# Attention values with both parts of V in one stationary operand, and the post-norm weights loaded when the norm chain begins

## The chip, the cores and the metric

The kernel runs on one core of a Trainium2 chip. The metric is the device time of one execution in microseconds (us), the median over several runs. The engines are TensorE (PE, with its weight loads listed apart as PEld), VectorE (DVE), ScalarE (ACT), GpSimd (POOL) and SyncE (SP), which issues most DMAs.

## What is computed

The reference is a trunk of two layers on 512 tokens of width 1024. Layer 0 has a pooling and state-space mixer, layer 1 has neighbourhood attention on a grid of 8 rows by 64 columns, and each layer has a feed-forward block ahead of the mixer or attention and one behind it. So there are six blocks in a row: ffn0, mixer, ffn1, ffn2, attention, ffn3. Every block is wrapped in two root-mean-square norms, and the second (the post-norm, with weights `norm_g[layer, k]`) is applied to the block's output before it is added to the residual stream:

```python
def rms_norm(x, g):
    y = xf * lax.rsqrt(jnp.mean(xf * xf, axis=-1, keepdims=True) + RMS_EPS)
    return (y * g.astype(F32)).astype(x.dtype)
...
        s = jnp.einsum('bqhd,biqjhd->bhqij', q_r, k_nb).astype(F32) + bias[None]
        p = jax.nn.softmax(s.reshape(bsz, N_HEADS, GRID_W, kh * KW), axis=-1)
...
        return jnp.einsum('bhqij,biqjhd->bqhd', p, v_nb)
```

There are 16 heads of 64 dimensions.

## The kernel before

**Products in parts.** Every fp32 matrix is split into a rounded part `hi` and a rest `lo`. A product is made of three products of parts, all summed in one PSUM bank: hi·hi, hi·lo and lo·hi (`mm3`, whose three lines are L170, L171 and L172). The split is made by `split_evac`: ACT copies PSUM into `hi` (L385), and DVE subtracts that from PSUM into `lo` (L386). With `later` the DVE half is put on a list and emitted afterwards. Weights come by DMA into `w_raw` (L74), ACT casts them to `w_hi` (L113), and DVE (or POOL) makes `w_lo` (L124).

**Attention.** Tokens stand in four query tiles of 128 for each head, so there are 64 units (head, tile `t`). A query tile sees a set of 192 or 256 keys, and its 128-key pieces are the two `CHUNKS` of the tile. One loop of 69 slots runs over the units as a pipeline. Slot by slot it emits, in this order: what `later` holds, `normalize` of the unit before, `values` of the unit five back, `transpose` of the unit three back, `scores` of this unit, one step of `spread` (evacuation of q and k), and then on average 1.35 filler steps on PE (`FILL_RATE`; projections of v, q and k for later heads, and products of the output projection, in banks `ps_f`). `scores` makes the logits in `ps_qk` (L883, L884), adds the bias, and takes the exponential; `transpose` turns the probabilities through PE (L907, bank `ps_pt`) and splits them into `pt_hi` and `pt_lo`; `values` multiplies them with `v_hi` and `v_lo` into `ps_o`. For each unit that is two chunks of three products with a 64-column stationary piece of V (one head) and 128 moving query columns. Some chunks have 64 keys, so that their products use 64 rows of the array. At `t == 3` the head's `ps_o` is split into `oT_hi` and `oT_lo`, the input of the output projection.

**The end of a block.** The output projection of a block is made in two halves of 512 columns: `ps_A` and then `ps_B` (in attention the first half stands in `ps_f` and `ps_o`). When the first half is done, a pool `chain` is allocated where the block's working tiles stood, and `chain_begin` takes the tile `fg` from it. `post_pair` sums the squares of each tile of 128 tokens on ACT (the tile `junk`) and multiplies it by `gpost` on DVE (`fg`, L242). Four more weight tiles (the tail) are split then, for the products of the second half, whose `fg` follow. Then come the residual, the norm of the next block, and its transposed input `xT_hi`, `xT_lo` (L319), on which the next block's products wait.

**The post-norm weights.** `load_gpost` broadcasts one row of 1024 weights to 128 partitions (512 KB in SBUF) by a DMA on SP's queue. It is called at the start of each block, and `gpost` stands in the pool `base`, which lives through the whole kernel.

Of the kernel before, what the change touches and what calls it, by code (L numbers as in the profile page):

```python
# [7 lines left out]
F32 = mybir.dt.float32  # L8
F32R = mybir.dt.float32r
# [6 lines left out]
P = 128  # L16
D = 1024
# [145 lines left out]
class Builder:  # L163
# [55 lines left out]

    def load_gpost(self, layer, k):  # L220
        self.gpost = self.base.tile([P, D], F32, tag="gpost", bufs=1, name="gpost")
        self.nc.sync.dma_start(self.gpost, self.ins["norm_g"][layer, k].partition_broadcast(P))
# [4 lines left out]

    def chain_begin(self, pool, scale):

        self.c_pool, self.c_scale = pool, 1.0 / (32.0 * scale)  # L230
        self.c_eps = EPS / (scale * scale)
        self.fg = pool.tile([P, TT, D], F32, name="fg")
        self.c_ss = {}
# [314 lines left out]
    def ffn(self, layer, which, gain, nxt, before, ssm=None):  # L548
# [5 lines left out]
        tc, nc, V = self.tc, self.nc, self.nc.vector  # L554
        self.load_gpost(layer, 1 if which == 0 else 5)
        n_plain = N_PLAIN[0 if ssm else 1]
# [188 lines left out]
    KEY0 = (0, 64, 192, 320)  # L745
    NKEY = (192, 256, 256, 192)

    CHUNKS = (((0, 64, 0, 64), (64, 128, 1, 0)), ((0, 128, 1, 0), (128, 128, 2, 0)),
              ((0, 128, 2, 0), (128, 128, 3, 0)), ((0, 128, 3, 0), (128, 64, 0, 0)))

    def attention(self, nxt, before):
        tc, nc, V = self.tc, self.nc, self.nc.vector
        ins = self.ins
        self.load_gpost(1, 3)
# [10 lines left out]
        def load_bias(head):  # L765
            bias[head] = z["ap"].tile([P, 4, 256], F32, tag="bias", bufs=2, name="bias")
            nc.sync.dma_start(bias[head], ins["att_bias"][head])
# [48 lines left out]
        def v_steps(c):  # L816

            pv = [self.bank("ps_f") for _ in range(2)]
            for i in range(2):
                w = self.W.take()  # L820
                for j in range(4):
                    kt = 4 * i + j
                    for s in range(4):
                        o = s % 2 * 256
                        self.mm3(pv[s // 2][:, o:o + 256], [keys(x[:, kt, :], s) for x in self.xT_all],
                                 [x[:, j * 256:(j + 1) * 256] for x in w], kt == 0 and s % 2 == 0,
                                 kt == KT - 1 and s % 2 == 1)
                    if kt < KT - 1:
                        yield
                if i == 0:  # L830
                    self.W.done()
            for b, ps in enumerate(pv):
                hi, lo = (x[:, 2 * b:2 * b + 2, c * 256:(c + 1) * 256] for x in vt)
                self.split_evac(hi, lo, ps.rearrange("p (s n) -> p s n", s=2), None, later)
            self.W.done()
            yield
# [38 lines left out]
        def scores(u):  # L875
            hp, a, t = u // 8, u // 4 % 2, u % 4
            rows, n = slice(64 * a, 64 * a + 64), self.NKEY[t]
            ps = self.bank("ps_qk")
            while u % 8 == 0 and spread:
                run_spread()  # L880
            tq = q[hp][a][:, t * P:(t + 1) * P]
            hi, lo = (x[:, self.KEY0[t]:self.KEY0[t] + n] for x in (k[hp][a], k[hp][2]))
            nc.tensor.matmul(ps[:, :n], tq, hi, start=True, stop=False)  # L883
            nc.tensor.matmul(ps[:, :n], tq[rows], lo[rows], start=False, stop=True)  # L884
            p = ap.tile([P, 256], F32, tag="p", bufs=5, name="p")
            m, s = self.small("att_m", 1), self.small("att_s", 1)
            V.tensor_tensor_reduce(out=p[:, :n], in0=ps[:, :n], in1=bias[2 * hp + a][:, t, :n], scale=-1.0,
                                   scalar=3e38, op0=ALU.add, op1=ALU.min, accum_out=m)
# [12 lines left out]
        def transpose(u):  # L901
            p, _ = st[u]
            ps = self.bank("ps_pt")
            pt = [ap.tile([P, 2, P], F32R, tag="pt" + n, bufs=2, name="pt" + n) for n in ("_hi", "_lo")]
            ch = self.CHUNKS[u % 4]
            for c, (o, n, _, _) in enumerate(ch):
                nc.tensor.transpose(ps[:n, c * P:(c + 1) * P], p[:, o:o + n], self.ident)  # L907
            if ch[0][1] == ch[1][1]:
                self.split_evac(pt[0], pt[1], ps[:, :256].rearrange("p (c n) -> p c n", c=2), None, later)
            else:  # L910
                for c, (_, n, _, r) in enumerate(ch):
                    self.split_evac(pt[0][r:r + n, c], pt[1][r:r + n, c], ps[:n, c * P:(c + 1) * P],
                                    None, later)
            st[u] = pt
# [404 lines left out]
    def mixer(self, nxt, before):  # L1319
        tc, nc, V, G = self.tc, self.nc, self.nc.vector, self.nc.gpsimd  # L1320
        ins = self.ins
        self.load_gpost(0, 3)
        xh, xl = self.xT
# [274 lines left out]
        cp = tc.alloc_tile_pool(name="chain", bufs=1)  # L1598
        self.chain_begin(cp, 1.0)
        out_a(range(TT), (4, 5))  # L1600
# [135 lines left out]
def lay_out(inputs):  # L1736
# [16 lines left out]
    for t in range(4):  # L1753
# [7 lines left out]
    bias = bias.reshape(16, 4, P, 256).transpose(0, 2, 1, 3)  # L1761

# [53 lines left out]
```

## Time and profile before

| what | value |
|---|---|
| median of three runs | 1896.97 us (1895.35 to 1897.27) |
| the profiled execution's own time | 1898.08 us |
| its span in the profile | 1896.3 us |
| granted TensorE clock, mean | 0.994 |
| PE busy | 1834.5 us, 97% |
| PEld busy | 1642.3 us, 87% |
| DVE busy | 1471.5 us, 78% |
| ACT busy | 925.5 us, 49% |
| POOL busy | 350.2 us, 18% |

Busy times are sums over the whole span. What an engine costs at one place has to be read from that place: an instruction's row has its start, its length, and in brackets the idle time of its engine before it and what ended that.

### The profile page before, as it was taken

To read this page: it belongs to the slowest core of one execution; us is meant where nothing else is said; L and a number is where in the kernel's file an instruction comes from. 1 tells how busy PE (TensorE), PEld (TensorE's weight loads), DVE (VectorE), ACT (ScalarE), POOL (GpSimd) and SP (SyncE) were. 2 spreads that over 40 slices of the span, in tenths; PEclk is the share of its full clock that TensorE was granted. 3 is DMA by queue.
4 is the path that set the end of the run, shared out by engine and by line. 5 is a ranking of instruction groups with operands and counts; after the bars stand their busy time and mean duration, and the time that the engine had idled before them with its cause. 6 is when DMAs were issued, how large, how long until landed. Compare 5 with 4: busy or idle time off the path is not lost.

```text
span 1896.3 us, 31539 instructions
## 1 busy us (share of the span) xinstructions
PE 1834.5 (97%) x12368; PEld 1642.3 (87%) x12368; DVE 1471.5 (78%) x2380; ACT 925.5 (49%) x1749; POOL 350.2 (18%) x238
## 2 busy tenths in 40 slices
PE   7999998998899999999999999999999999999998
PEld 7877996887679999988899998889878789999886
DVE  5788989968769999854899996465565579999744
ACT  5344446365455454543644445355555565444532
POOL 2021231014011223200132330002222012322100
PEclk9999999999999999999999999999999999999999
DMA  5365336637532333332233323223222132333321
GB/s 195 127 198 188 101 123 199 206 120 253 172 123 79 101 112 101 106 115 80 79 111 104 108 90 133 90 78 129 85 99 100 57 111 90 101 112 101 122 93 64
DMA packets 82021, 225.48 MB, mean 119 GB/s; under 512 B 15792, under 2 KB 20048, under 8 KB 80848
## 3 DMA queue, kind: packets, MB, share of 16 engines
q1 hardware_dynamic: 70176, 197.80, 31.0%
q0 software_dynamic: 6960, 23.57, 4.1%
q10 hardware_dynamic: 4736, 2.10, 0.4%
q8 instruction: 97, 1.59, 0.3%
q14 instruction: 52, 0.43, 0.1%
HBM read 206.69 MB, written 18.84 MB: 119 GB/s over the span
## 4 chain that ended last, share of the span: by engine, by line
PE 65%; DVE 5%; ACT 3%; issue 1%; DMA 1%; DVEq 0%; ACTq 0%
PE ps_gu L172 10%; PE ps_gu L171 10%; PE ps_gu L170 10%; PE ps_A L170 3%; PE ps_A L172 3%; PE ps_A L171 3%; PE ps_B L172 3%; PE ps_B L171 3%; PE ps_B L170 3%; PE ps_f L170 3%; PE ps_f L171 2%; PE ps_f L172 2%; PE ps_qk L884 1%; ACT junk L226 1%; DVE w_lo L124 1%
## 5 line engine op out<-in xcount | busy, mean ns | idle before, releaser
L124 DVE TENSOR_TENSOR w_lo<-w_raw,w_hi 128x1024 fp32r<-128x1024 f32 x214 | 283.4, 1330 | 210.7 <-ACT w_hi L113 210.6
L113 ACT CAST w_hi<-w_raw 128x1024 fp32r<-128x1024 f32 (+1 forms) x313 | 262.8, 864 | 264.5 <-PE ps_A L172 73.7
L172 PE MATMUL ps_gu<-xsum,w_lo 128*128 128x256 f32 x1088 | 308.1, 283 | 0.8 <-DVE w_lo L124 0.8
L171 PE MATMUL ps_gu<-xsum,w_hi 128*128 128x256 f32 x1088 | 308.2, 283 | 0.3 <-DVE xsum L505 0.3
L172 PE MATMUL ps_gu<-xT_hi,w_lo 128*128 128x256 f32 (+1 forms) x1008 | 307.1, 305 | 1.4 <-DVE w_lo L124 1.4
L170 PE MATMUL ps_gu<-xsum,w_hi 128*128 128x256 f32 x1088 | 307.8, 283 | 0.0
L170 PE MATMUL ps_gu<-xT_hi,w_hi 128*128 128x256 f32 (+1 forms) x1008 | 304.9, 303 | 0.0
L171 PE MATMUL ps_gu<-xT_lo,w_hi 128*128 128x256 f32 (+1 forms) x1008 | 304.6, 302 | 0.0
L172 PEld LDWEIGHTS ps_gu<-xsum,w_lo 128*128 128x128 f32 x1088 | 208.8, 192 | 0.9 <-DVE w_lo L124 0.9
L171 PEld LDWEIGHTS ps_gu<-xsum,w_hi 128*128 128x128 f32 x1088 | 208.6, 192 | 0.7 <-DVE xsum L505 0.7
L170 PEld LDWEIGHTS ps_gu<-xsum,w_hi 128*128 128x128 f32 x1088 | 208.6, 192 | 0.0
L172 PEld LDWEIGHTS ps_gu<-xT_hi,w_lo 128*128 128x128 f32 x1008 | 190.5, 189 | 12.7 <-DVE w_lo L124 2.2
L170 PEld LDWEIGHTS ps_gu<-xT_hi,w_hi 128*128 128x128 f32 x1008 | 190.4, 189 | 8.5 <-issue 0.9
L171 PEld LDWEIGHTS ps_gu<-xT_lo,w_hi 128*128 128x128 f32 x1008 | 190.3, 189 | 7.3
L98 POOL TENSOR_TENSOR w_u<-w_raw,w_s 128x512 f32<-128x512 f32 x64 | 112.2, 1753 | 360.9 <-ACT w_hi L113 196.3
L124 POOL TENSOR_TENSOR w_lo<-w_raw,w_hi 128x1024 fp32r<-128x1024 f32 x31 | 74.0, 2389 | 564.0 <-ACT w_hi L113 533.9
L113 ACT CAST w_hi<-w_s 128x512 fp32r<-128x512 f32 x136 | 77.8, 623 | 197.8 <-DVE w_s L96 192.8
L96 DVE TENSOR_TENSOR w_s<-w_raw,w_u 128x1024 f32<-128x1024 f32 x68 | 145.8, 2144 | 2.4
L172 PE MATMUL ps_A<-w_hi,gT 128*128 128x512 f32 x352 | 138.3, 393 | 5.7 <-DVE gT L678 5.7
L625 POOL TENSOR_TENSOR g<-g,m 128x1024 f32<-128x1024 f32 x34 | 94.6, 2781 | 245.0 <-DVE m L623 245.0
L170 PE MATMUL ps_A<-w_hi,gT 128*128 128x512 f32 x352 | 138.0, 392 | 1.1 <-DVE m L620 1.1
L171 PE MATMUL ps_A<-w_lo,gT 128*128 128x512 f32 x352 | 137.8, 392 | 0.0
(376 smaller groups left out, 4259.0 us busy)
## 6 DMA issues: line engine op xcount, KB each, us to landing
w_raw<-in_w_gu_dram SPq DMA_DIRECT2D x106, 512.0 KB, 3.3
w_raw<-in_w_dn_dram SPq DMA_DIRECT2D x88, 512.0 KB, 3.2
w_u<-in_w_gu_dram SPq DMA_DIRECT2D x70, 512.0 KB, 3.7
w_raw<-in_w_qk_dram SPq DMA_DIRECT2D x16, 512.0 KB, 3.2
bias<-in_att_bias_dram SPq DMA_DIRECT2D x16, 512.0 KB, 4.1
w_raw<-in_w_in_dram SPq DMA_DIRECT2D x8, 512.0 KB, 3.2
cm<-m_dram SPq DMA_DIRECT2D x4, 1024.0 KB, 8.0
w_raw<-in_w_ao_dram SPq DMA_DIRECT2D x8, 512.0 KB, 3.8
```

Of the source, the lines that this page charges most:

```text
L96: tt(out=blocks(s), in0=g[:, :HALF].unsqueeze(1).broadcast_to([P, 2, HALF]), in1=blocks(u)[:, :2], op=ALU.subtract)
L98: (h_engine or self.nc.gpsimd).tensor_tensor(out=u[:, :HALF], in0=g[:, HALF:], in1=s[:, HALF:], op=ALU.add)
L113: self.nc.scalar.copy(hi[:, k:k + step], src[:, k:k + step])
L124: (engine or self.lo_engine).tensor_tensor(out=lo[:, :n], in0=src, in1=hi[:, :n].bitcast(F32), op=ALU.subtract)
L170: mm(ps, a[0], b[0], start=start, stop=False)
L171: mm(ps, a[0], b[1], start=False, stop=False)
L172: mm(ps, a[1], b[0], start=False, stop=stop)
L226: self.nc.scalar.activation(out=junk[:, :src.shape[-1]], in_=src, func=AF.Square, scale=scale, accum_out=out)
L625: nc.gpsimd.tensor_tensor(out=rows(f), in0=rows(f), in1=m, op=ALU.mult)
L884: nc.tensor.matmul(ps[:, :n], tq[rows], lo[rows], start=False, stop=True)
```

## The change

**Values.** The two parts of V for one head now lie side by side in one tile `v`, so that one stationary operand of 128 columns holds `v_hi` and `v_lo`. The probabilities' parts `pt_hi` and `pt_lo` of a head stay in one tile of eight chunks. A key set that two query tiles use serves both in one product with 256 moving columns. So `values` emits nothing at `t == 0` and `t == 2`, four products at `t == 1` and six at `t == 3`: ten for a head, where there were 24. Rows 0 to 63 of the bank then hold the v_hi sums and rows 64 to 127 the v_lo sums (the product lo·lo is now among them). ACT copies the upper half to a new tile `o_sum`, DVE adds the lower half to it one slot later (L950 of the changed kernel), and the split into `oT_hi` and `oT_lo` follows from `o_sum`, its DVE part one more slot later. `run_later` runs only what was on the list when it began.

**Sizes.** The bias tile is 896 columns wide where it was 1024, and the tile `p` has four buffers where it had five.

**Post-norm weights.** `load_gpost` is called by `chain_begin`, and `gpost` is the first tile of the chain's pool. In attention `chain_begin` now stands before the last out products of the first half.

```diff
-    def load_gpost(self, layer, k):
-        self.gpost = self.base.tile([P, D], F32, tag="gpost", bufs=1, name="gpost")
+    def load_gpost(self, pool, layer, k):
+        self.gpost = pool.tile([P, D], F32, name="gpost")
         self.nc.sync.dma_start(self.gpost, self.ins["norm_g"][layer, k].partition_broadcast(P))
...
-    def chain_begin(self, pool, scale):
+    def chain_begin(self, pool, scale, *gain):
+        self.load_gpost(pool, *gain)
...
-        self.load_gpost(layer, 1 if which == 0 else 5)
...
-        self.chain_begin(cp, 0.5)
+        self.chain_begin(cp, 0.5, layer, 1 if which == 0 else 5)
...
         def run_later():
-            while later:
-                later.pop(0)()
+            now = later[:]
+            del later[:]
+            for f in now:
+                f()
...
-        vt = [ap.tile([P, TT, D], F32R, name=n) for n in ("v_hi", "v_lo")]
+        vt = ap.tile([P, TT, 16, 2, 64], F32R, name="v")
+        pt = [ap.tile([P, 8, P], F32R, name="pt" + n) for n in ("_hi", "_lo")]
...
         def values(u):
             hp, a, t = u // 8, u // 4 % 2, u % 4
-            if t == 0:
-                st["o"] = self.bank("ps_o")
-            o = st["o"]
-            pt = st.pop(u)
-            d0 = (2 * hp + a) * 64
-            for c, (_, n, s, r) in enumerate(self.CHUNKS[t]):
-                self.mm3(o[:64, t * P:(t + 1) * P], [x[r:r + n, s, d0:d0 + 64] for x in vt],
-                         [x[r:r + n, c] for x in pt], c == 0, c == 1)
-            if t == 3:
+            if t == 1:
+                o = st["o"] = self.bank("ps_o")
+            elif t == 3:
+                o = st.pop("o")
+            else:
+                return
+            head = vt[:, :, 2 * hp + a].rearrange("p s i d -> p s (i d)")
+            def product(rows, s, chunks, first=False):
+                n = len(chunks) * P
+                at = chunks[0] // 2 * P
+                for i, x in enumerate(pt):
+                    nc.tensor.matmul(o[:, at:at + n], head[rows, s],
+                                     x[rows, chunks[0]:chunks[-1] + 1].rearrange("p c n -> p (c n)"),
+                                     start=first and i == 0, stop=chunks[-1] == 7 and i == 1)
+            if t == 1:
+                product(slice(0, 128), 1, (1, 2), True)
+                product(slice(64, 128), 0, (0,))
+                return
+            product(slice(0, 128), 3, (5, 6))
+            product(slice(0, 128), 2, (3, 4))
+            product(slice(0, 64), 0, (7,))
+            w = ap.tile([P, SEQ], F32, tag="o", bufs=1, name="o_sum")[64 * a:64 * a + 64]
+            nc.scalar.copy(w, o[64:])
+            def rest():
+                V.tensor_tensor(out=w, in0=o[:64], in1=w, op=ALU.add)
                 hi, lo = (x[64 * a:64 * a + 64, hp, :].rearrange("p (r c) -> p r c", r=8) for x in oT)
-                self.split_evac(hi, lo, o[:64].rearrange("p (c r) -> p r c", r=8), None, later)
+                self.split_evac(hi, lo, w.rearrange("p (c r) -> p r c", r=8), None, later)
+            later.append(rest)
...
-        run_later()
+        while later:
+            run_later()
...
         cp = tc.alloc_tile_pool(name="chain", bufs=1)
+        self.chain_begin(cp, 1.0, 1, 3)
         for _ in out_steps((0, 1, 2), (KT - 1,)):
             pass
-        self.chain_begin(cp, 1.0)
```

The order of PE's products in one slot of the attention loop, before the change (a slot whose unit has one chunk of full rows and one of 64 keys for the transposes):

```order
L172 MATMUL ps_f<-xT_hi,w_lo 128x512
L170 MATMUL ps_o<-pt_hi,v_hi 64x128
L171 MATMUL ps_o<-pt_lo,v_hi 64x128
L172 MATMUL ps_o<-pt_hi,v_lo 64x128
L170 MATMUL ps_o<-pt_hi,v_hi 64x128
L171 MATMUL ps_o<-pt_lo,v_hi 64x128
L172 MATMUL ps_o<-pt_hi,v_lo 64x128
L907 MATMUL ps_pt<-ident,p 128x128
L907 MATMUL ps_pt<-ident,p 64x128
L883 MATMUL ps_qk<-k_13980,q_13866 128x256
L884 MATMUL ps_qk<-k_lo,q_13866 128x256
```

The same engine in a slot with `t == 3`, of the changed kernel:

```order
L172 MATMUL ps_f<-xT_hi,w_lo 128x512
L935 MATMUL ps_o<-pt_hi,v 128x256
L935 MATMUL ps_o<-pt_lo,v 128x256
L935 MATMUL ps_o<-pt_hi,v 128x256
L935 MATMUL ps_o<-pt_lo,v 128x256
L935 MATMUL ps_o<-pt_hi,v 128x128
L935 MATMUL ps_o<-pt_lo,v 128x128
L911 MATMUL ps_pt<-ident,p 128x128 x2
L887 MATMUL ps_qk<-k_13151,q_13121 128x192
L888 MATMUL ps_qk<-k_lo,q_13121 128x192
```

The six products of one unit, which occurred in each of four slots, have become six products of twice the width or of 64 rows in one slot, and four in another; the products around them keep their order.

DVE at the end of attention, before the change, from the last values to the first `fg`:

```order
L386 TENSOR_TENSOR pt_lo<-ps_pt,pt_hi 128x128
L386 TENSOR_TENSOR pt_lo<-ps_pt,pt_hi 64x128
L386 TENSOR_TENSOR oT_lo<-ps_o,oT_hi 64x512
L242 TENSOR_TENSOR fg<-ps_f,gpost 128x512 x2
L124 TENSOR_TENSOR w_lo<-w_raw,w_hi 128x1024 x4
```

And of the changed kernel:

```order
L387 TENSOR_TENSOR pt_lo<-ps_pt,pt_hi 128x128
L387 TENSOR_TENSOR pt_lo<-ps_pt,pt_hi 64x128
L950 TENSOR_TENSOR o_sum<-ps_o,o_sum 64x512
L387 TENSOR_TENSOR oT_lo<-o_sum,oT_hi 64x512
L243 TENSOR_TENSOR fg<-ps_f,gpost 128x512 x2
L124 TENSOR_TENSOR w_lo<-w_raw,w_hi 128x1024 x4
```

One addition stands ahead of the last `oT_lo`, and the `fg` behind it now need a `gpost` whose transfer is issued here.

SP's queue at the end of the mixer, before the change (`y` is read back from DRAM for the mixer's output products; `w_ao` are their weights, `w_gu` those of ffn1):

```order
L1445 DMA y<-y_dram 128x512
L74 DMA w_raw<-in_w_ao_dram 128x1024 x4
L74 DMA w_raw<-in_w_gu_dram 128x1024 x5
L71 DMA w_u<-in_w_gu_dram 128x2x512
L74 DMA w_raw<-in_w_gu_dram 128x1024
```

And of the changed kernel:

```order
L1471 DMA y<-y_dram 128x512
L74 DMA w_raw<-in_w_ao_dram 128x1024 x4
L222 DMA gpost<-in_norm_g_dram 128x1024
L74 DMA w_raw<-in_w_gu_dram 128x1024 x5
L71 DMA w_u<-in_w_gu_dram 128x2x512
```

The mixer's `gpost` transfer, which was issued at the block's start, now stands behind the last four loads of `w_ao`, each of which waits for a free `w_raw` buffer.

In the changed kernel the instruction for which the `gpost` transfer waits, in the four feed-forward blocks, is the last DVE instruction that writes `gT` (L678 in the kernel before), since `gpost` now takes the memory of tiles that the block used to the end. In attention it is the last `oT_lo`. In the mixer it is a product far ahead of the block's end.

## Rows read from the trace of the kernel before

**Rows 1.** The page: busy time, share and instructions of each engine.

```profile
PE 1834.5 (97%) x12368; PEld 1642.3 (87%) x12368; DVE 1471.5 (78%) x2380; ACT 925.5 (49%) x1749; POOL 350.2 (18%) x238
```

**Rows 2.** Windows, attention loop: us; PE, PEld, DVE, ACT, POOL busy; PEclk; DMA; GB/s.

```profile
1305.00:1504.00 199.00, 198.24 (x1262) 158.69 (x1262) 117.97 (x396) 111.97 (x301) 45.09 (x19) 1.00 0.27 91
```

**Rows 3.** Timeline of PE: start, length, line, out<-in, rows*columns, shape, count.

```profile
1341.22 0.40 PE L172 MATMUL ps_f<-xT_hi,w_lo 128*128 128x512 f32 x1
...
1342.10 0.29 PE L907 MATMUL ps_pt<-ident,p 128*128 128x128 f32 x1
...
1344.35 0.22 PE L170 MATMUL ps_o<-pt_hi,v_hi 128*64 128x128 f32 x1
...
1344.71 0.40 PE L907 MATMUL ps_pt<-ident,p 128*128 128x128 f32 x2
1344.87 0.36 PE L883 MATMUL ps_qk<-k,q 128*128 128x256 f32 x1
...
1345.47 0.50 PE L170 MATMUL ps_f<-xT_hi,w_hi 128*128 128x512 f32 x1
...
1350.68 0.39 PE L172 MATMUL ps_f<-xT_hi,w_lo 128*128 128x512 f32 x1
1350.90 0.22 PE L170 MATMUL ps_o<-pt_hi,v_hi 128*64 128x128 f32 x1
...
1351.18 0.27 PE L170 MATMUL ps_o<-pt_hi,v_hi 64*64 64x128 f32 x1
...
1351.50 0.33 PE L907 MATMUL ps_pt<-ident,p 128*128 128x128 f32 x1
```

**Rows 4.** Timeline of ACT, DVE and PE at the end of attention.

```profile
1503.10 0.58 ACT L385 CAST oT_hi<-ps_o 64x512 fp32r<-64x512 f32 x1 [1.88 <-PE ps_o L172]
1503.71 0.68 DVE L386 TENSOR_TENSOR oT_lo<-ps_o,oT_hi 64x512 fp32r<-64x512 f32 x1 [1.98 <-ACT oT_hi L385]
1504.49 0.40 PE L170 MATMUL ps_f<-w_hi,oT_hi 128*128 128x512 f32 x1
...
1506.09 1.29 DVE L242 TENSOR_TENSOR fg<-ps_f,gpost 128x512 f32<-128x512 f32 x2 [1.69 <-PE ps_f L172]
1508.54 2.36 DVE L124 TENSOR_TENSOR w_lo<-w_raw,w_hi 128x1024 fp32r<-128x1024 f32 x2 [1.16 <-ACT w_hi L113]
...
1512.19 0.39 PE L170 MATMUL ps_B<-w_hi,oT_hi 128*128 128x512 f32 x1
```

**Rows 5.** The tile gpost: its six transfers, from issue to landing.

```profile
DMA to landing us min/median/max: 4.1/4.3/4.9
```

**Rows 6.** Timeline of SP's queue, DVE and PE at the mixer's end.

```profile
510.17 21.20 SPq L74 DMA_DIRECT2D w_raw<-in_w_ao_dram  x4
...
534.32 1.23 DVE L124 TENSOR_TENSOR w_lo<-w_raw,w_hi 128x1024 fp32r<-128x1024 f32 x1 [2.11 <-ACT w_hi L113]
537.89 1.23 DVE L124 TENSOR_TENSOR w_lo<-w_raw,w_hi 128x1024 fp32r<-128x1024 f32 x1 [1.15 <-ACT w_hi L113]
...
541.27 0.40 PE L171 MATMUL ps_B<-w_lo,xT_hi 128*128 128x512 f32 x1
```

**Rows 7.** Timeline of DVE and PE from the end of ffn0 into the mixer.

```profile
381.65 2.49 DVE L678 TENSOR_TENSOR gT<-g,gT 128x512 fp32r<-128x512 f32 x4
...
388.05 1.23 DVE L124 TENSOR_TENSOR w_lo<-w_raw,w_hi 128x1024 fp32r<-128x1024 f32 x1 [0.96 <-ACT w_hi L113]
389.89 0.69 DVE L242 TENSOR_TENSOR fg<-ps_B,gpost 128x512 f32<-128x512 f32 x1 [0.61 <-PE ps_B L172]
...
402.87 0.39 PE L171 MATMUL ps_p<-xT_lo,w_hi 128*128 128x256 f32 x1 [0.27 <-DVE xT_lo L319]
```

**Rows 8.** Timeline of DVE at the end of ffn1.

```profile
897.55 0.69 DVE L242 TENSOR_TENSOR fg<-ps_B,gpost 128x512 f32<-128x512 f32 x1 [6.46 <-PE ps_B L172]
```

**Rows 9.** Windows at the start of ffn2: an idle stretch of PE, and the one behind it.

```profile
925.55:927.65 2.10, 0.00 (x0) 0.00 (x0) 2.10 (x4) 0.00 (x0) 0.00 (x0) 1.00 0.00 0
928.10:931.10 3.00, 3.00 (x16) 3.00 (x16) 2.54 (x6) 2.78 (x9) 0.00 (x0) 0.50 0.93 333
```

More of the change, by code (lines that the diff above doesn't have):

```diff
@@ L746 @@
     NKEY = (192, 256, 256, 192)
+    BIAS0 = (0, 192, 448, 704)
     CHUNKS = (((0, 64, 0, 64), (64, 128, 1, 0)), ((0, 128, 1, 0), (128, 128, 2, 0)),
@@ L753, in attention @@
         ins = self.ins
-        self.load_gpost(1, 3)
         q, k, bias, later, spread, z = {}, {}, {}, [], [], {}
         def run_later():
-            while later:
-                later.pop(0)()
+            now = later[:]
+            del later[:]
+            for f in now:
+                f()
         def run_spread():
@@ L765, in load_bias @@
         def load_bias(head):
-            bias[head] = z["ap"].tile([P, 4, 256], F32, tag="bias", bufs=2, name="bias")
+            bias[head] = z["ap"].tile([P, 896], F32, tag="bias", bufs=2, name="bias")
             nc.sync.dma_start(bias[head], ins["att_bias"][head])
@@ L832, in v_steps @@
             for b, ps in enumerate(pv):
-                hi, lo = (x[:, 2 * b:2 * b + 2, c * 256:(c + 1) * 256] for x in vt)
-                self.split_evac(hi, lo, ps.rearrange("p (s n) -> p s n", s=2), None, later)
+                hi, lo = (vt[:, 2 * b:2 * b + 2, 4 * c:4 * c + 4, i] for i in range(2))
+                self.split_evac(hi, lo, ps.rearrange("p (s h d) -> p s h d", s=2, h=4), None, later)
             self.W.done()
@@ L884, in scores @@
             nc.tensor.matmul(ps[:, :n], tq[rows], lo[rows], start=False, stop=True)
-            p = ap.tile([P, 256], F32, tag="p", bufs=5, name="p")
+            p = ap.tile([P, 256], F32, tag="p", bufs=4, name="p")
             m, s = self.small("att_m", 1), self.small("att_s", 1)
-            V.tensor_tensor_reduce(out=p[:, :n], in0=ps[:, :n], in1=bias[2 * hp + a][:, t, :n], scale=-1.0,
+            V.tensor_tensor_reduce(out=p[:, :n], in0=ps[:, :n], in1=bias[2 * hp + a][:, self.BIAS0[t]:self.BIAS0[t] + n], scale=-1.0,
                                    scalar=3e38, op0=ALU.add, op1=ALU.min, accum_out=m)
@@ L901, in transpose @@
         def transpose(u):
-            p, _ = st[u]
+            p, _ = st.pop(u)
             ps = self.bank("ps_pt")
-            pt = [ap.tile([P, 2, P], F32R, tag="pt" + n, bufs=2, name="pt" + n) for n in ("_hi", "_lo")]
-            ch = self.CHUNKS[u % 4]
+            t = u % 4
+            ch = self.CHUNKS[t]
             for c, (o, n, _, _) in enumerate(ch):
@@ L908, in transpose @@
             if ch[0][1] == ch[1][1]:
-                self.split_evac(pt[0], pt[1], ps[:, :256].rearrange("p (c n) -> p c n", c=2), None, later)
+                self.split_evac(*(x[:, 2 * t:2 * t + 2] for x in pt),
+                                ps[:, :256].rearrange("p (c n) -> p c n", c=2), None, later)
             else:
                 for c, (_, n, _, r) in enumerate(ch):
-                    self.split_evac(pt[0][r:r + n, c], pt[1][r:r + n, c], ps[:n, c * P:(c + 1) * P],
-                                    None, later)
@@ L914, in transpose @@
-            st[u] = pt
+                    self.split_evac(*(x[r:r + n, 2 * t + c] for x in pt), ps[:n, c * P:(c + 1) * P], None, later)
         def values(u):
             hp, a, t = u // 8, u // 4 % 2, u % 4
-            if t == 0:
-                st["o"] = self.bank("ps_o")
-            o = st["o"]
-            pt = st.pop(u)
-            d0 = (2 * hp + a) * 64
-            for c, (_, n, s, r) in enumerate(self.CHUNKS[t]):
-                self.mm3(o[:64, t * P:(t + 1) * P], [x[r:r + n, s, d0:d0 + 64] for x in vt],
-                         [x[r:r + n, c] for x in pt], c == 0, c == 1)
@@ L1321, in mixer @@
         ins = self.ins
-        self.load_gpost(0, 3)
         xh, xl = self.xT
@@ L1598, in mixer @@
         cp = tc.alloc_tile_pool(name="chain", bufs=1)
-        self.chain_begin(cp, 1.0)
+        self.chain_begin(cp, 1.0, 0, 3)
         out_a(range(TT), (4, 5))
@@ L1760, in lay_out @@
                 bias[:, t, :, r, :, i] = rpb[:, i - r + 7][:, dc]
-    bias = bias.reshape(16, 4, P, 256).transpose(0, 2, 1, 3)
+    bias = bias.reshape(16, 4, P, 256)
+    bias = np.concatenate([bias[:, t, :, :n] for t, n in enumerate(Builder.NKEY)], axis=2)
     edge = np.zeros((4, 16), np.float32)
```

## Prediction, on record before the changed kernel ran

> **What bounds the kernel now.** I read the busy times first, to see which engine has no room. PE is busy 1834.5 us, 97% of the span; DVE, the next, has 78% [rows 1]. A share over the whole span says nothing of a stage, so I then read the windows of the attention loop, where the values stand: in 199.00 us PE is busy 198.24, DVE 117.97 and ACT 111.97, at a granted clock of 1.00 [rows 2]. There PE's products follow each other without a wait, and a product saved is time saved; DVE and ACT have about 80 us of room for additions. Third I read PE's timeline inside that loop, start to start, since the lengths in its rows overlap [rows 3]. Last, the ends of the blocks, because the post-norm weights are used there: the first fg of a block, what released it, and whether DVE stood idle before the fg of the second half [rows 4, 6 to 8].
>
> **The change, part by part.** All prices come from one execution with a time of its own of 1898.08 us.
>
> *Values on PE.* A filler product of 512 columns takes 0.22 us to the next product (1350.68 to 1350.90), so 256 columns take 0.12 and 128 columns 0.06 as I round it. Before, for one head [rows 3]: at t=0 from the last filler to the transpose 0.88 (1341.22 to 1342.10), less the filler's own 0.22, so 0.66; at t=1 0.36 (1344.35 to 1344.71), six products of 0.06, so that a change from 128 to 64 columns costs nothing; t=2 has the same two full chunks, so 0.36 again; at t=3 0.60 (1350.90 to 1351.50). Together 1.98 us for a head.
>
> After it: six products with 256 columns, 6 × 0.12 = 0.72, and four of 64 rows with 128 columns, in two visits. A visit to 64 rows and back is not free. At t=3 the three full products take 0.28 and not 0.18 before the first of 64 rows starts, and the three of 64 rows 0.32 and not 0.18: 0.24 for the visit. The scores' pair, one of full rows and one of 64, takes 0.60 (1344.87 to 1345.47) where two products of 256 columns take 0.24: 0.36 for the visit. So each visit costs 0.24 to 0.36 and 2 × 0.06 for its products, two visits 0.72 to 0.96, and a head 1.44 to 1.68. The new operand is 128 columns wide, like that of the scores, so I stand nearer to the upper end: 1.60. That saves 0.38 a head, over 16 heads **−6.0 us**. No row before shows 128 moving columns on a 64-row operand of 128 columns. If such a product takes as long as one of 256 columns, 0.06 more for each of four, a head takes 1.92 and the saving is 1.0; at the lower end it is 8.6.
>
> The Trainium skill, "TensorE: Matmul & The Clock Gate", section "LDWEIGHTS (loading the stationary operand)", says that a load's time goes with the columns of the stationary operand, columns divided by 1.2 in ns. That is 53 ns for 64 columns and 107 for 128, which speaks against the wide operand under narrow products: four products at 0.107 in place of 0.06 would make a head 1.79 and the saving 3.0. That the six products at t=1 run at 0.06 each agrees with it for 64 columns [rows 3]; no row here has 128 columns under so narrow a product.
>
> *Values off PE.* A head adds one ACT copy of 64 by 512, priced by the cast of that shape, 0.58, and one DVE addition, priced by the subtraction of that shape, 0.68 [rows 4]: 9.3 and 10.9 us over the loop, beside PE, where both have some 80 us idle [rows 2]. If there were no such room, they would cost the sum. What can be late is a split of probabilities or a bank behind them in the one slot with t=3, whose PE work grew; I take **+0.5**, between 0 and 2. The narrower bias shortens a transfer that nothing waits for in that loop, and one buffer of p less still leaves four for a pipeline that is three units deep: 0.
>
> *The end of attention.* Before, the last cast took 0.58, oT_lo 0.68, and the product that needs them started at 1504.49 [rows 4]. Now the copy (0.58), the addition (0.68), the cast (0.58) and oT_lo (0.68) follow each other. The two added steps are 1.26; the cast needs no wait for products that follow, and the first out products need only oT_hi, so that 0.8 of them is seen by PE. The gpost transfer is issued only behind the last oT_lo, at 1504.39 + 1.26, so about 1505.7; it lands 4.1 to 4.9, in the median 4.3, later [rows 5], near 1510.0, where the first fg started at 1506.09 before. From the start of that fg to the end of the first w_lo it was 3.63 (1506.09 to 1508.54, and half of 2.36): 1513.6. The second product of ps_B needs it at 1512.19 + 0.22 + the 0.8 from above = 1513.2. So 0.4 more there, and about 0.5 at the later tail tiles, whose work on ACT and DVE has moved with it: **+1.75**, between 1.0 and 2.8.
>
> *The mixer.* The transfer waits for nothing late by itself, but on SP's queue it is behind four loads of w_ao, the last of which SP issues at 531.37 (510.17 + 21.20) [rows 6]. It lands 4.3 to 4.9 later, at 535.7 to 536.3. With the 3.63 from fg to w_lo of the end of attention [rows 4], the third tail weight is ready at 539.3 to 539.9, and the fourth, 3.57 behind it as before (534.32 to 537.89) [rows 6], at 542.9 to 543.5. PE took it at 541.27. That is 1.6 to 2.2; **+2.1**, since ACT's work of the tail is shifted too, between 1.0 and 3.2.
>
> *The end of ffn0.* The transfer waits for the last gT, which ends at 384.14 (381.65 + 2.49) [rows 7]. The first fg stood right behind it and now waits 4.1 to 4.9, in the median 4.3 [rows 5]. Behind fg on DVE stand the weights' w_lo and the fg of ps_B, and before that one DVE was idle for only 0.61 [rows 7]. So fg of ps_B is some 3.6 late. From there the residual, the norm and xT_lo follow without slack: the product at 402.87 waited 0.27 for xT_lo already [rows 7]. **+3.5**, between 2.5 (4.1 less the idle 0.61 and the 0.96 before w_lo) and 4.3 (4.9 less 0.61).
>
> *ffn1, ffn2, ffn3.* The same wait, but DVE is idle 6.46 us before the fg of ps_B in ffn1 [rows 8], which swallows 4.3; ffn2 and ffn3 have the same order of work. **0**; if the shift there went through ACT to the tail's weights, 1 us each, which is in the upper end of my range. The earlier loads that are dropped at the blocks' starts held up nobody: 0.
>
> A page bears on the terms with gpost. The Trainium skill, "DMA: Bandwidth & Descriptors", section "Anatomy of one DMA", fits a transfer as 2.0 us and its bytes by 436 GB/s, an estimate of 3.2 us for 512 KB, where the rows show 4.1 to 4.9 [rows 5]; by it each of the three waits would be 1.1 us shorter, and the sum 3.3 lower. Its "Rules for kernel authors" say to issue a transfer early and wait for it late, which this part of the change undoes.
>
> **Sum.** −6.0 + 0.5 + 1.75 + 2.1 + 3.5 = +1.85 on 1898.08, so 1899.9 in the state of that execution. It stood 1.1 above the median, so **1898.9 us**. With all terms at their lower ends it is −8.6 + 0 + 1.0 + 1.0 + 2.5 = −4.1, at their upper ends −1.0 + 2.0 + 2.8 + 3.2 + 4.3 + 3 = +14.3.
>
> **Rivals.** A difference of 0.2%, 3.8 us, is about what a measurement of this kernel can tell from no change: faster is below 1893.2, slower above 1900.8.
>
> *The waits are absorbed, and only the products count.* The three ends of blocks have other work of PE beside them, and the trace may show a wait where an engine would have waited for something else. For it: three blocks have 6 us of idle on DVE at that place [rows 8]. Against it: ffn0 has 0.61, and its next product already waits for the chain [rows 7]. Time: 1896.97 − 6.0 + 0.5 = 1891.5.
>
> *The products are not cheaper.* Where the wide operand's load is not hidden, or each visit to 64 rows takes longer than 0.36, a head stays at 1.98. The point from which this decides is 1.85 a head (a saving of 2): with the waits of 7.85 the kernel is then clearly slower. For it: a 64-row visit already costs 0.36 in the scores [rows 3]. Against it: there were as many visits before, and 24 products become 10. Time: 1896.97 + 7.85 = 1904.8. This is the rival on the other side.
>
> *The clock.* In ffn2 PE stood idle for 2.10 us, and in the stretch of 3.00 us behind it the granted clock was 0.50, which is 1.2 of its 2.4 GHz [rows 9]; that cost 1.5 us. At the end of ffn0 the change makes a gap of over 3 us where there was 0.27. If the clock falls behind it in the same way, 1.5 is added once: 1900.4, and with a second one at another block's end 1901.9; I take 1901.
>
> **How the numbers follow.** My sum has a chance of 0.52, with a range of its own from 1896 to 1901.2; absorbed waits 0.13; products not cheaper 0.10; the clock 0.25. Faster: nearly all of the absorbed case and a little of the sum's lower tail, 0.14. Slower: the dear products, somewhat over half of the clock case, and 0.06 of the sum's upper tail, 0.30. The rest, 0.56, is within 0.2%. The range from 1893.0 to 1904.0 leaves out about half of each of the first and second rival and little else, some 2 in 10.
>
> **What would show it.** In the attention loop ten products for each head and a start-to-start sum near 1.6 us; below 1.4 or above 1.9 that term is wrong. At the end of ffn0 the first fg released by the transfer some 4.3 us behind the last gT, the fg of ps_B at about 393.5, and a PE wait of about 3.8 for xT_lo or what stands ahead of it. At the mixer's end the last tail weight at about 543. In attention the first fg at about 1510 less what the loop saved. In ffn1, ffn2 and ffn3 an fg that is late and a PE that does not wait. The prediction is wrong if the fg of ps_B in ffn0 is not late, if the loop shrinks by under 2 or over 9 us, or if DVE or ACT ends PE's waits inside the loop.

## The result: slower by 0.6%, and the profile after

The changed kernel takes 1910.3 us (median of 4, 1905.33 to 1911.28), the kernel before 1897.01. The ratio is 1.0062, with an interval from 1.0046 to 1.0077: 13 us slower, outside the range that was forecast.

The profiled execution after has a span of 1908.8 us, 12.5 more than before, and a mean granted clock of 0.987, where it was 0.994. It is the slowest of the four; the fastest, 1905.33 us, had 0.991. The page's first rows of the changed kernel, to be held against [rows 1]:

```profile
PE 1840.5 (96%) x12144; PEld 1646.2 (86%) x12144; DVE 1488.5 (78%) x2396; ACT 945.3 (50%) x1765; POOL 350.4 (18%) x238
```

PE has 224 products fewer and is busy 6.0 us longer. That points to products that ran at a lower clock, so waits alone do not explain the result. To find the places I took products that both programs have and compared their starts (us), in PE's two timelines. A step in the difference is time lost (or won) between two of them:

| product | before | after | difference | step |
|---|---|---|---|---|
| ffn0, ps_A | 289.90 | 289.54 | −0.36 | |
| ffn0, ps_B | 379.94 | 381.53 | 1.59 | +1.95 |
| ffn0, ps_B, late | 398.07 | 399.66 | 1.59 | 0 |
| mixer, first projections | 406.08 | 409.93 | 3.85 | +2.26 |
| mixer, ps_A | 520.01 | 523.55 | 3.54 | −0.31 |
| mixer, ps_B, token tile 1 | 533.33 | 542.34 | 9.01 | +5.47 |
| mixer, ps_B, 50 products on | 545.00 | 556.90 | 11.90 | +2.89 |
| attention loop, start | 1305.08 | 1316.94 | 11.86 | −0.04 |
| attention loop, near its end | 1477.09 | 1485.55 | 8.46 | −3.40 |
| attention loop, 7 us on | 1483.98 | 1495.05 | 11.07 | +2.61 |
| last slots of the loop | 1499.77 | 1509.78 | 10.01 | −1.06 |
| end of attention | 1506.12 | 1518.32 | 12.20 | +2.19 |
| ps_B of attention | 1529.92 | 1542.60 | 12.68 | +0.48 |
| ffn3, ps_B | 1880.02 | 1892.56 | 12.54 | −0.14 |

**The mixer's end**, 8.4 us in two steps. Before, DVE's first fg and PE's first product of ps_B for token tile 1 started without a wait:

```profile
530.93 1.28 DVE L242 TENSOR_TENSOR fg<-ps_A,gpost 128x512 f32<-128x512 f32 x2
...
533.33 0.40 PE L170 MATMUL ps_B<-w_hi,xT_hi 128*128 128x512 f32 x1
```

SP's queue, DVE, ACT and PE there, in the changed kernel's timeline:

```profile
513.21 21.71 SPq L74 DMA_DIRECT2D w_raw<-in_w_ao_dram  x4
535.02 0.38 SPq L222 DMA_DIRECT2D gpost<-in_norm_g_dram  x1
...
540.82 1.29 DVE L243 TENSOR_TENSOR fg<-ps_A,gpost 128x512 f32<-128x512 f32 x2 [6.25 <-DMA gpost<-in_norm_g_dram]
...
541.60 0.60 ACT L226 ACTIVATE junk<-ps_A 128x512 bf16<-128x512 f32 x1 [7.96 <-DVE fg L243]
...
542.34 0.80 PE L170 MATMUL ps_B<-w_hi,xT_hi 128*128 128x512 f32 x1 [5.30 <-ACT junk L226]
```

The transfer is issued directly behind the fourth load of w_ao, as foreseen, but the first fg starts 5.80 us later, where [rows 5] had 4.9 at most. Then PE: it does not wait for a tail weight. It waits 5.30 us for ACT's second sum of squares, which waits for fg, and both read the bank that ps_B of token tile 1 takes over. Windows of the same stretch (us; PE, PEld, DVE, ACT, POOL busy; PEclk; DMA share; GB/s):

```profile
537.00:542.30 5.30, 0.04 (x1) 0.00 (x0) 1.29 (x2) 0.70 (x3) 0.00 (x0) 0.94 0.45 178
542.30:549.00 6.70, 6.66 (x17) 5.22 (x18) 3.77 (x5) 4.18 (x7) 0.00 (x0) 0.54 0.27 81
549.00:552.00 3.00, 3.00 (x15) 2.40 (x13) 1.10 (x1) 0.00 (x0) 0.00 (x0) 1.00 0.82 254
```

After the idle stretch PE runs 6.70 us at a granted clock of 0.54, nearly the lower of its two levels (1.2 GHz). That is the second step, 2.89.

**The end of ffn0.** DVE, then PE, in the timeline of the changed kernel:

```profile
382.01 2.49 DVE L678 TENSOR_TENSOR gT<-g,gT 128x512 fp32r<-128x512 f32 x4
388.54 1.89 DVE L243 TENSOR_TENSOR fg<-ps_A,gpost 128x512 f32<-128x512 f32 x3 [4.04 <-DMA gpost<-in_norm_g_dram]
...
393.57 1.28 DVE L243 TENSOR_TENSOR fg<-ps_B,gpost 128x512 f32<-128x512 f32 x2
...
403.34 1.94 PE L298 MATMUL ps_t<-ident,xn 128*128 128x128 f32 x16 [1.02 <-issue]
...
405.79 0.39 PE L170 MATMUL ps_p<-xT_hi,w_hi 128*128 128x256 f32 x1 [0.51 <-ACT xT_hi L319]
406.55 0.39 PE L171 MATMUL ps_p<-xT_lo,w_hi 128*128 128x256 f32 x1 [0.37 <-DVE xT_lo L320]
```

The wait of 4.04 is there, and fg of ps_B is at 393.57, where the prediction had 393.5 (389.89 in [rows 7]). The product that waits for xT_lo is late by the same 3.68 (406.55, 402.87 in [rows 7]). PE stood idle for less, 1.02 + 0.51 + 0.37 in place of 0.27, because it came to this place 1.59 late itself, by half-clock stretches in ffn0 (below).

Four kernels of the experiments have the same ffn0 (the post-norm move alone, the mixer's weights early, PE occupied, another order), and in their profiled executions PE came here between 0.10 early and 0.56 late against before. There it is idle for 2.9 to 3.2 us ahead of the transposes, and loses 4.0 to 4.2 from the late ps_B product to the one that waits for xT_lo. In the first of them:

```profile
403.76 1.94 PE L298 MATMUL ps_t<-ident,xn 128*128 128x128 f32 x16 [3.13 <-issue]
...
406.96 0.39 PE L171 MATMUL ps_p<-xT_lo,w_hi 128*128 128x256 f32 x1 [0.37 <-DVE xT_lo L320]
```

So the steps of 1.95 and 2.26 in the table are not two costs to be added up. By these traces the late fg sets when PE goes on, and what PE lost in ffn0 went into that wait.

**The loop.** Two transposes two heads apart start at 1380.46 and 1406.48 before, and after:

```profile
1390.65 0.38 PE L911 MATMUL ps_pt<-ident,p 128*128 128x128 f32 x2
...
1399.47 0.28 PE L935 MATMUL ps_o<-pt_hi,v 128*128 128x256 f32 x1
...
1400.04 0.33 PE L935 MATMUL ps_o<-pt_hi,v 64*128 64x128 f32 x1
1400.20 0.27 PE L935 MATMUL ps_o<-pt_lo,v 64*128 64x128 f32 x1
1400.40 0.44 PE L911 MATMUL ps_pt<-ident,p 128*128 128x128 f32 x2
...
1406.29 0.27 PE L935 MATMUL ps_o<-pt_hi,v 128*128 128x256 f32 x1
...
1406.97 0.44 PE L911 MATMUL ps_pt<-ident,p 128*128 128x128 f32 x2
...
1416.01 0.38 PE L911 MATMUL ps_pt<-ident,p 128*128 128x128 f32 x2
```

A visit at t=3 takes 0.93 (1399.47 to 1400.40) and one at t=1 0.68 (1406.29 to 1406.97): 1.61 a head, against the 1.60 of the prediction. Two heads take 25.36 where they took 26.02: 0.33 won for each, 5.3 over 16 if all are like these two. Against that stand PE's waits in the loop and behind it (columns: who waits for whom, us in total, times, longest), of the changed kernel from 1290 to 1530 us:

```profile
PE ps_qk L887 <- DVE att_m L891: 1.6, 4, 0.8
PE ps_f L170 <- ACT oT_hi L386: 0.9, 1, 0.9
PE ps_qk L887 <- ACT k L792: 0.5, 1, 0.5
PE ps_f L172 <- DVE oT_lo L387: 0.4, 1, 0.4
```

`att_m` is written by DVE's addition of the bias to the scores, which reads `ps_qk`. Before, the same view has one row, 0.8 for att_m. Two of the changed kernel's waits are followed by a stretch at a lower clock:

```profile
1487.89 0.35 PE L887 MATMUL ps_qk<-k,q 128*128 128x192 f32 x1 [0.50 <-ACT k L792]
...
1489.91 0.39 PE L887 MATMUL ps_qk<-k,q 128*128 128x256 f32 x1 [0.27 <-DVE att_m L891]
```

```profile
1490.00:1494.00 4.00, 4.00 (x11) 2.94 (x12) 3.36 (x10) 2.44 (x7) 0.00 (x0) 0.57 0.60 235
```

**The end of attention.** ACT and DVE of the changed kernel, against [rows 4]:

```profile
1513.43 0.58 ACT L947 COPY o_sum<-ps_o 64x512 f32<-64x512 f32 x1 [1.76 <-PE ps_o L935]
1514.04 0.68 DVE L950 TENSOR_TENSOR o_sum<-ps_o,o_sum 64x512 f32<-64x512 f32 x1 [1.86 <-ACT o_sum L947]
1514.76 1.11 ACT L386 CAST oT_hi<-o_sum 64x512 fp32r<-64x512 f32 x1 [0.75 <-DVE o_sum L950]
1515.91 1.10 DVE L387 TENSOR_TENSOR oT_lo<-o_sum,oT_hi 64x512 fp32r<-64x512 f32 x1 [1.18 <-ACT oT_hi L386]
1521.08 1.29 DVE L243 TENSOR_TENSOR fg<-ps_f,gpost 128x512 f32<-128x512 f32 x2 [4.07 <-DMA gpost<-in_norm_g_dram]
```

The copy and the addition cost what was forecast, but the cast and the subtraction, which read the permuted tile from SBUF now, take 1.11 and 1.10 where they took 0.58 and 0.68 from PSUM. Over all 16 heads they take 1.20 and 1.27 in the mean, against 0.58 and 0.68.

**Stretches at half clock in unchanged code.** The first step of the table, 1.95, lies in ffn0's down projection, whose instructions are the same. After, the granted clock there is 0.50 from 299.4 to 302.7 and from 326.7 to 330.0; before, it is 0.50 from 313.6 to 316.9 alone. In ffn1 PE waits 2.19 us for xT_lo in both programs, before until 574.13 and after until 586.19. Before, the windows from 574 to 577 and from 577 to 580 have a clock of 1.00. After:

```profile
586.20:589.40 3.20, 3.20 (x15) 3.20 (x16) 2.86 (x7) 2.99 (x8) 0.00 (x0) 0.50 0.53 164
```

The same wait is followed by half clock in one execution and not in the other. The difference between the timelines grows by 0.71 there, from 12.06 to 12.77, and is back at 12.04 at 712 us of before: this stretch cost the kernel nothing in the end. At the start of ffn2 the lower clock follows the wait in both traces (right behind it in [rows 9], 1.2 us on after). So which of the short waits is followed by half clock differs from trace to trace, and it is not a cost of any one instruction. It takes no other program: of two profiled executions of one kernel (those of "All first halves early" below) one has a clock of 0.50 from 472.8 to 476.1 and the other of 1.00, and at the end of ffn0 they lie 1.2 us apart.

### The profile page after: what moved, and what is told of

It is laid out like the page before. It is cut to its first block, busy times and chain, and to the rows that moved or that the text cites. A ratio compares the mean times of both kernels' runs of the same rounds, so it can differ in the third digit from the quotient of the medians.

```text
span 1908.8 us, 31103 instructions
## 1 busy us (share of the span) xinstructions
PE 1840.5 (96%) x12144; PEld 1646.2 (86%) x12144; DVE 1488.5 (78%) x2396; ACT 945.3 (50%) x1765; POOL 350.4 (18%) x238
## 4 chain that ended last, share of the span: by engine, by line
PE 63%; DVE 6%; ACT 3%; DMA 2%; issue 1%; DVEq 0%; ACTq 0%; SPq 0%
PE ps_gu L172 10%; PE ps_gu L171 10%; PE ps_gu L170 10%; PE ps_A L170 3%; PE ps_A L171 3%; PE ps_A L172 3%; PE ps_B L170 3%; PE ps_B L171 3%; PE ps_B L172 3%; PE ps_f L170 2%; PE ps_f L172 2%; PE ps_f L171 2%; PE ps_o L935 1%; DVE w_lo L124 1%; ACT junk L226 1%
```

## Experiments

Theory A was that the move of the post-norm weights makes the loss: a wait for a bank at the mixer's end, the lowered clock behind it, and smaller waits in ffn0 and attention. Theory B was that the new values cost the time. Each kernel was timed beside the kernel before; medians of "before" in these runs are 1897.56 to 1898.35 us.

**The post-norm move alone.** The kernel before with this part of the change only (the second line of the diff that is added stands in `chain_begin`; the calls at the blocks' starts go):

```diff
-        self.gpost = self.base.tile([P, D], F32, tag="gpost", bufs=1, name="gpost")
+        self.gpost = pool.tile([P, D], F32, name="gpost")
...
+        self.load_gpost(pool, *gain)
```

> The kernel before with the post-norm weights loaded when the chain begins, values untouched. Theory A (the loss is made by this move: mixer's end 5.2 us of waiting and about 3.5 of a lowered clock behind it, ffn0's end about 2, attention's end about 1, and some more stretches at half clock): 1907 to 1912 us. Theory B (the new values cost the time, the move is cheap as in the prediction's terms for ffn0 and mixer at their lower ends): 1900 us or less.

Measured: 1911.51 us, ratio 1.0065 (1.0053 to 1.0078). The whole loss is there without the new values. Against before, its timeline has 4.2 us at ffn0's end, 5.71 and 2.75 at the mixer's, and 0.1 over the attention loop. Its waits of PE from 525 to 560 us show the bank:

```profile
PE ps_B L170 <- ACT junk L226: 5.5, 1, 5.5
```

Theory B falls. This ratio and that of the changed kernel, 1.0062, differ by less than either's interval: net, the new values gave the changed kernel nothing that can be measured.

**The mixer's weights early.** The changed kernel, with the first 512 columns of the weights loaded when the mixer's working pool is made, and only the rest by `chain_begin`:

```diff
+            self.early_gpost(yp, 0, 3)
...
+            late = pool.tile([P, HALF], F32, name="gpost")
```

> The changed kernel, but the mixer's first half of the post-norm weights is loaded at the mixer's start into its own pool; the other blocks as changed. Theory A (at the mixer's end PE waits 5.2 us for a bank whose sum of squares waits for the transfer, and then runs 6.8 us at half clock): 8 to 9 us less than the changed kernel, 1901 to 1903 us. Rival (the mixer's term is about 2 as predicted and the rest is luck of the clock elsewhere): 1907 to 1909 us.

Measured: 1899.89 us, ratio 1.0009 (1.0 to 1.0018), 10.4 us below the changed kernel and 1 us below the expected range. PE waits for no bank there, and from 541 to 548 us:

```profile
541.00:548.00 7.00, 7.00 (x31) 5.63 (x30) 2.84 (x3) 2.57 (x4) 0.00 (x0) 1.00 0.58 188
```

The table gives 8.4 for this place, and this timeline has no step there at all against before. The other 2 us were not traced; executions of one kernel differ by as much.

**The wait kept, PE occupied.** The changed kernel with 24 added products:

```diff
         tail = [self.W.take() for _ in range(4)]
+        for _ in range(8):
+            self.rows(psB[0], lhs, 0, 0, tail[0], 0, True, True)
```

> The changed kernel, with 24 products of 512 columns (5.3 us) put ahead of the mixer's second half, into a bank that the first real product overwrites: PE has work while it would have waited. Theory A (the clock falls because PE stood idle): the transfer is as late as before, but the 6.8 us at half clock behind it are gone, 3 to 4 us less than the changed kernel, about 1907 us. Rival (the clock falls there for another reason, for instance the transfers): no less than 1910 us.

Measured: 1907.33 us, ratio 1.0042 (1.003 to 1.0055), 3.0 below the changed kernel though it does more work. The transfer is as late as before (DVE waits 6.35 us for it), PE has no idle time, and the clock stays up:

```profile
537.00:542.30 5.30, 5.30 (x24) 4.25 (x24) 0.27 (x1) 0.00 (x0) 0.00 (x0) 1.00 0.66 216
542.30:549.00 6.70, 6.70 (x30) 5.27 (x29) 4.39 (x6) 3.84 (x8) 0.00 (x0) 1.00 0.23 78
```

Against before, its timeline has 0.06 where the changed kernel's has 2.89. So the second step at the mixer's end is the idle time's and not the transfers'.

**Another order of the products there.** The first two tail weights serve token tile 0 in full first:

```diff
-        for i in range(n):
+        for t in (0, 1):
+            for i in range(lead):        # 4 in the mixer
+                product(i, t)
+        for i in range(lead, n):
             for t in (0, 1):
                 product(i, t)
```

> The changed kernel, with another order of the products at the mixer's end: the first two tail weights serve token tile 0 in full (12 products) before token tile 1 starts (12 products), where the two tiles took turns. If PE waits there for the second bank, which the late fg holds, 9 products of 0.22 us move into the wait: it falls from 5.3 to about 3.3 us, 1908 us, or about 1905 if the clock does not fall behind it. Rival (PE waits there for a late tail weight, as the prediction priced it): the wait only moves, 1910 us.

Measured: 1907.09 us, ratio 1.0047 (1.0034 to 1.0059), 3.2 below the changed kernel. The wait fell by about the length of the nine products, and it is still for the bank:

```profile
542.32 0.80 PE L170 MATMUL ps_B<-w_hi,xT_hi 128*128 128x512 f32 x1 [3.37 <-ACT junk L226]
```

The clock fell behind this wait too. A late tail weight, which the prediction priced, is not what PE waits for.

**ffn0's weights early.** The changed kernel with `early_gpost` in a pool of its own ahead of ffn0's down projection.

> The changed kernel, but in ffn0 the first half of the post-norm weights is loaded ahead of the down projection, into a pool of its own; all else as changed. By the two traces PE lost 2.2 us there: 1908 us, if the clock behind it does not change. By the prediction's term of 3.5: 1907 us. Rival (the waits in ffn0 only move a later wait): no less than 1910 us.

Measured: 1905.41 us, ratio 1.0039 (1.0026 to 1.0051), 4.9 below the changed kernel, more than either number. By the two timelines 2.2 of it lies between the end of ffn0's products and the mixer's first ones (399.66 to 409.93 in the changed kernel, 396.20 to 404.25 here), where PE's one wait is 0.3 us; against before, this place has no step. 2.4 us were won ahead of 290 us already, where the products are the same. The 2.2 is so small because PE was late in the changed kernel's profiled execution; the 4.0 to 4.2 that the four other kernels lose here are nearer to the 4.9.

**All first halves early, and no tile for the sum.** This is the changed kernel with theory A's cause removed. The early call stands in the mixer and in attention too; `down` is rows 0 to 63 of the bank, `up` rows 64 to 127, and `hi` and `lo` are the head's parts of oT_hi and oT_lo:

```diff
+        self.early_gpost(self.base, layer, 1 if which == 0 else 5)
...
-            nc.scalar.copy(w, o[64:])
+            nc.scalar.copy(hi, down)
+            nc.scalar.copy(lo, up)
...
-                V.tensor_tensor(out=w, in0=o[:64], in1=w, op=ALU.add)
+                V.tensor_tensor(out=down, in0=down, in1=hi.bitcast(F32), op=ALU.subtract)
+                V.tensor_tensor(out=lo, in0=down, in1=lo.bitcast(F32), op=ALU.add)
```

> The changed values, with the first half of the post-norm weights loaded at the start of every block into the pool that lives through the kernel, and only the second half loaded when the chain begins. To make room, the sum of the two halves of the bank is not kept in a tile of its own: ACT rounds the lower half into oT_hi and the upper half into oT_lo, DVE subtracts in PSUM and adds into oT_lo. Theory A (the values save 5 us, the waits of the weights were all of the loss): 1891 to 1895 us, faster than before. Rival (the values gain nothing, the loop's waits and the clock eat it): 1897 us or more.

Measured: 1896.53 us, ratio 0.999 (0.9981 to 0.9999); and once more:

> The kernel with all first halves loaded early and no tile for the sum, once more beside the one above on the same chip. If its 0.1% gain over the kernel before is real, 1895 to 1898 us and at most 0.1% either way from what it showed; if it was luck of the clock, its interval reaches above 1.001.

Measured: 1895.98 us, ratio 0.9992 (0.9983 to 1.0001), as expected of a gain that is real. The loss is gone, but the gain is 0.1% and not the 3 to 7 us of the expectation, and the time is nearer to the rival's. Waits of PE from 1290 to 1520 us in the first of the two:

```profile
PE ps_qk L901 <- DVE att_m L905: 2.8, 4, 0.9
PE ps_f L173 <- DVE oT_lo L967: 0.7, 1, 0.7
PE ps_o L949 <- DVE pt_lo L399: 0.2, 1, 0.2
```

That is 3.7 us against 0.8 before: of the 5.3 that the products save, some 2.9 are spent again on waits. From the loop's start to ps_B of attention the two timelines show 0.7 won in each of the two executions, so 1.7 more of the 5.3 is not accounted for.

**Where the loop's waits come from.** Three kernels built on this one. First, ACT's second copy and DVE's second operation one slot later each:

> As the kernel with all first halves loaded early and no tile for the sum, but ACT's copy of the upper half is put one slot later, and of DVE's two operations the second one slot after the first. If the loop's waits for the scores' sums (2.8 us there against 0.8 before) come from ACT's and DVE's additions standing in one slot with an evacuation of q or k, they fall to about 1, and the time is 1893 to 1896 us. Rival (they come from the order of the products on PE, which is unchanged): 1896 to 1898 us.

Measured: 1899.41 us (1893.74 to 1902.65), ratio 1.0006 (0.9997 to 1.0015). The wait for att_m fell to 1.0, but one for ACT's k of 1.0 came up, and in the profiled execution the clock fell at 1480 us. It is no better, and slower than both ranges of the expectation. Second, no step of q or k in slots with t=3:

> As the kernel with all first halves loaded early and no tile for the sum, but no step of an evacuation of q or k is emitted in the slots with t=3, where ACT copies both halves of the bank. If the loop's waits for the scores' sums (2.8 us in that kernel) come from DVE waiting for ACT's q or k cast behind those two copies, they fall to 1 us or less and the time is about 2 us less than that kernel's: 1893 to 1896 us. Rival (the waits come from elsewhere): no less, 1896 to 1899 us.

Measured: 1896.13 us, ratio 0.9989 (0.9981 to 0.9998), and 2.5 us of waits for att_m left: the waits hardly fell. The trace shows that the edit missed the place:

```profile
1349.60 0.58 ACT L962 CAST oT_hi<-ps_o 64x512 fp32r<-64x512 f32 x1
1350.19 0.58 ACT L963 CAST oT_lo<-ps_o 64x512 fp32r<-64x512 f32 x1
1350.80 0.37 ACT L398 CAST pt_hi<-ps_pt 128x256 fp32r<-128x256 f32 x1
1351.19 0.59 ACT L401 ACTIVATE q<-ps_f 64x512 fp32r<-64x512 f32 x1
...
1351.82 0.69 DVE L402 SCALAR_TENSOR_TENSOR q<-ps_f,q 64x512 fp32r<-64x512 f32 x1 [2.43 <-ACT q L401]
1352.55 0.36 DVE L905 CUSTOM_DVE_ANT_0 p<-ps_qk,bias 128x192 f32<-128x192 f32 x1
```

ACT still casts q behind both copies, since `scores` finishes an open evacuation when a pair of heads begins, and this slot has t=3. DVE stands 2.43 us at q's rest, with the scores' sum behind it. Third, that evacuation is finished ahead of the values:

```diff
             run_later()
+            while slot % 8 == 0 and spread:
+                run_spread()
```

> As the kernel with all first halves loaded early and no tile for the sum, but an evacuation of q that is still open when a new pair of heads begins is finished at the start of that slot, ahead of the values, where the scores of that slot forced it behind ACT's two copies before (skipping a step of spread could not change that: the scores force it). If PE's waits for the scores' sums come from that place, 2.5 to 2.8 us of them become 1 us or less, and the time is 1 to 2 us less than that kernel's: 1893 to 1896 us. Rival (they come from the order on DVE alone): waits of 2 us or more remain, 1895 to 1898 us.

Measured: 1894.94 us, ratio 0.9986 (0.9976 to 0.9995), the best version. Its waits for att_m from 1285 to 1520 us are

```profile
PE ps_qk L901 <- DVE att_m L905: 1.9, 3, 0.9
```

Less, and not the 1 us expected: the place is one cause of them, and what makes the other three waits was not tried. No trace shows a wait for one of the fewer buffers of `p`: from 1305 to 1500 us, in the changed kernel and in the first of "All first halves early", the instruction that writes it waits for `ps_qk` alone. Its gain over the version without the edit, 1.0 to 1.6 us between medians, is no larger than the intervals; from the loop's start to ps_B of attention its timeline won 1.9 against before, where that version won 0.7.

## Why the prediction was wrong

The sum had +1.85, and the two spans differ by 12.5. Of the 10.7 that it lacks, 6.3 are at the mixer's end and 3.7 in the attention loop.

**The mixer's term failed**, the step "The mixer": it went by the tail weights alone, as "PE took it at 541.27", and gave +2.1. PE's wait was for the second bank of ps_B, which fg and the sum of squares behind it still held, 5.30 us, and the transfer took longer (5.80 to fg, not 4.3 to 4.9; that the load of w_ao just ahead of it is why was not tried). Measured: +5.47 for the wait ([rows 6] against the rows above; the early load and the other order of products both remove what this says they should) and +2.89 for the clock behind it.

**The clock was put too low**, the rival "The clock": the mechanism was right, its places and its price were not. Behind the mixer's wait it cost 2.89 (shown by the occupied PE; 2.75 in the post-norm move alone), where the sum had nothing and the rival 1.5. Behind ffn0, where the rival expected it first, no half-clock stretch followed in the changed kernel. In three of the four other kernels with that ffn0 one did (clocks of 0.60 to 0.68 from 404 to 408), and still the product that waits for xT_lo was no later than fg of ps_B by more than 0.1, so it cost little there. In the loop it cost 1.7 of the +2.61 (0.57 for 4 us). That is bad luck: three of the four other kernels with the same attention code (the mixer's weights early, PE occupied, another order) had no such stretch there. A chance of 0.25 and 1.5 us were too little for a change that makes gaps of 5 us. The rival that the products are no cheaper had a time of 1904.8, but not for the reason that held.

**The loop's term failed by the prediction's own signs.** It shrank by 1.85 (−3.40 + 2.61 − 1.06), where the sum had 5.5 and "under 2" was to show it wrong, and DVE and ACT ended PE's waits inside it. The values' products: 1.61 us a head where the sum had 1.60, a saving of 5.3 where it had 6.0. The two narrow products of a visit start 0.16 apart (1400.04, 1400.20), so the visit's price is in them as much as at its ends. The Trainium skill, "TensorE: Matmul & The Clock Gate", section "LDWEIGHTS (loading the stationary operand)", divides a load's columns by 1.2, an estimate of 107 ns for 128 columns. The trace has more than that between these two, but the 1.79 a head that the prediction got by adding it to its visits was not reached. The loop's stalls: waits of 2.1 against 0.8, 1.3 where the sum had 0.5. With the 1.7 of the clock that leaves some 0.4 open.

**The other terms.** ffn0 was right: fg was as late as forecast to a tenth, and so was the product behind it. The table's 1.95 + 2.26 make 4.21 from 289.90 on, and the four other kernels lose 4.0 to 4.2 there, where the sum had 3.5, at most 4.3. The transfers took 3.6 to 5.6 us, in the median 3.8. The prediction's estimate of 3.2 us for them is by a fit that the Trainium skill, "DMA: Bandwidth & Descriptors", section "Anatomy of one DMA — SWDGE (gpsimd) path", gives for transfers that GpSimd issues; these are SP's. The end of attention: 2.19 + 0.48 where the sum had 1.75, within its bounds. 1.3 of it are PE's waits for oT_hi and oT_lo, which the slower reads of `o_sum` lengthen; the prediction priced both by reads from PSUM. ffn1, ffn2 and ffn3 at 0 were right on balance: from the mixer's last ps_B to the loop the table has −0.04, and for ffn3 −0.14.

With the measured sizes: 4.21 for ffn0 and its end, 5.47 + 2.89 for the mixer's, −3.40 + 2.61 − 1.06 for the loop, 2.67 for the end of attention, −0.85 for the rest (−0.36 at the start among it), 12.5 in all, as the two spans say.

## What to carry to other kernels

A load that is moved to where its tile's memory comes free is late by its own duration plus what its queue puts ahead of it. Ask what every late reader holds, and not only when the next weights come: an accumulator that the late instruction reads keeps its PSUM bank, and PE stops at the bank. Where a wait leaves PE idle for some us, price the clock behind it as a second term, and put real products into the gap if the wait can't be removed. Loading only the half that is needed first, early, cost half the memory here and took away all of the wait.

## What was not expected of the hardware

The same wait of 2.19 us in unchanged code was followed by 3.20 us at half clock in one execution and by none in the other. Ahead of 290 us, where all have the same products, the kernels' timelines lie between 2.8 us ahead of before (ffn0's weights early) and 1.3 us behind it (the post-norm move alone), so a difference of 1 to 3 us between two kernels is not yet an effect of the edit. A cast and a subtraction of 64 by 512 took 1.11 and 1.10 us with a permuted source in SBUF, against 0.58 and 0.68 with the permuted source in PSUM.
